# A kernel of two transformer blocks: normed rows turned and split by halves, and the next residual made later on VectorE

## The chip, the cores and the metric

The kernel runs on one core of a Trainium2 chip. The metric is the device time of one execution in microseconds (us). The engines are called as the profile calls them: PE is TensorE (the matmuls), PEld its loads of stationary operands, DVE VectorE, ACT ScalarE, POOL GpSimd, SP SyncE, which issues the DMAs. L408 is line 408 of the kernel before.

## The reference

Two blocks follow each other on one sequence of 512 tokens with 1024 columns. In the first, each of two layers computes `hcat = x @ w_in + b_in`, three attention or gating branches out of it, and then

```python
sub = merged @ w_out + b_out
return layer_norm(DEEPNORM_ALPHA * x + sub, ln_g, ln_b)
```

The second block has two layers of

```python
p = jnp.einsum('btd,dc->btc', h, w_in[l]).astype(F32)
...                                     # four recurrent mixers on p
h = _layer_norm(DN_ALPHA * h + mix, ln1_g[l], ln1_b[l])
f = _swiglu(h, ...)                     # l = 0; a mixture of experts at l = 1
h = _layer_norm(DN_ALPHA * h + f, ln2_g[l], ln2_b[l])
```

So a layer norm stands between any two stages: its result is the input of the next stage's matmuls, and, times `ALPHA` (plus the next layer's `b_out` in the first block), the residual that the next norm adds.

## The kernel before, in words

The rows `H` lie on chip as four row tiles `t` of 128 tokens in two halves `j` of 512 columns, each 128x512 in float32. There are six places at which a norm's result goes into a next stage; I number them by time in the trace: 1, the input of the first layer (from 14.2 us); 2, the second layer (607 us); 3, the mixers of the second block (1192 us); 4, the FFN (`swiglu`, 1620 us); 5, the mixers again (1993 us); 6, the router and experts (2426 us). The last norm goes to the output.

At such a place `norm_rows` does a row tile at a time as its sums arrive: the statistics, the power -0.5 on POOL (L439), and `norm_apply`: the half `j` = 0 in two DVE operations (L467, L468), the half `j` = 1 by ACT (L355), POOL (L470) and DVE (the bias, L485). `norm_end` (L498) then transposes (`norm_transpose`, L495: 32 of 128x128) into seven banks of the accumulator memory and an eighth once one is free, and splits each of the eight transposed columns `k` (128x512) into a high part `hh`, rounded to the matmul's format by ACT (L414), and the rest `hl`, by DVE (L415). After the splits it makes the residual: sixteen multiplications by `ALPHA` at places 1 and 2 (8 each) and eight at each of the others on ACT (L515), and at places 1 and 2 sixteen additions of the bias on POOL (L518) and a store of each into `hd` (SP, L520).

A projection, `proj_f` (L420), takes one bank ("mm", of which there are two) and adds up 24 matmuls of 128x512, three for each `k`: `hh`·`wh`, `hl`·`wh`, `hh`·`wl` (L406, L407, L408). Its operation that reads the bank (the evacuation) is DVE's L592 in the first block, `shift` (ACT L1530, DVE L1532 to L1534) in the mixers, and Silu on ACT (L355) or a DVE multiplication in the FFN. The weights come in chunks of 128x1024 (256 columns, four `k`): a DMA into `wr` (L394), a cast into `wh` by ACT (L395), the rest into `wl` by DVE (L399). A weight of two outputs is thus two chunks, `k` 0 to 3 and `k` 4 to 7. There are four buffers of each.

The order on every engine comes from the framework's scheduler, which takes the program as it is written and puts instructions where it expects them ready; each engine then works strictly in its order. One thing is ordered by hand: in front of a stage, `behind` lets the first `wl` of the next weights go as it will (`FREE = 1`), and orders the next ones behind a split, that of `k` = 3 (`BEHIND`).

Of the kernel before, what the change touches and what calls it, by code (L numbers as in the profile page):

```python
# [314 lines left out]
class K:  # L315
    def __init__(self, ctx, tc, aps):
        self.tc, self.nc, self.aps = tc, tc.nc, aps
        self.ctx = ctx
        pool = lambda name, **kw: ctx.enter_context(tc.tile_pool(name=name, **kw))
        self.cp = pool("cp", bufs=1)  # L320
        self.wp = pool("wp", bufs=2)
        self.xp = pool("xp", bufs=1)
        self.ps = pool("ps", bufs=2, space=PSUM)
        self.dp = pool("dp", bufs=1, space=bass.MemoryType.DRAM)
        nc = self.nc
        x = [[lambda t=t, j=j: self.load(aps["x"][t * P:(t + 1) * P, j * S:(j + 1) * S], "H") for j in range(2)]
             for t in range(4)]
# [12 lines left out]
        nc.vector.memset(self.eps_rms, RMS_EPS)  # L340
        self.mhalf = self.cp.tile([P, 1], F32, name="mhalf")
        nc.vector.memset(self.mhalf, -0.5)
        self.log_exp = False
        self.behind = (None, 0, 0)
        self.hd = [self.dp.tile([S, S], F32, name=f"hd{j}") for j in range(2)]
# [81 lines left out]

    def proj_t(self, w, width, t, hT, kt=KT, tag="mm"):
# [13 lines left out]
    def norm_begin(self, ng, nb, bo=None, keep=None, spill=False, tags="tsatsamt", pool=()):  # L442
# [3 lines left out]
                                  keep=keep, spill=spill, tags=banks, tp={}, pool=pool, late=None,  # L446
# [4 lines left out]
    def norm_rows(self, t, st, apply=True):  # L451
# [4 lines left out]
        with self.tc.issue_after(i):  # L456
            self.norm_late()
        nc.vector.scalar_tensor_tensor(ln.sh[:, t:t + 1], ln.mv[:, t, 0:1], -1.0, ln.rs[:, t:t + 1],
# [31 lines left out]
    def norm_transpose(self, t, ks=range(7)):  # L490
        ln = self.ln
        for k in ks:
            if k not in ln.tp:
                ln.tp[k] = self.bank(ln.tags[k])
            self.nc.tensor.transpose(ln.tp[k][:, t * P:(t + 1) * P], self.H[t][k // 4][:, (k % 4) * P:(k % 4 + 1) * P],  # L495
                                     self.ident)

    def norm_end(self):  # L498

        nc, ln, H = self.nc, self.ln, self.H  # L500
        hh = self.xp.tile([P, KT, S], F32R, name="hh", tag="hh")
        hl = self.xp.tile([P, KT, S], F32R, name="hl", tag="hl")
        for t in range(4):
            self.norm_transpose(t)
        for k in range(KT):
            if k >= 7:
                for t in range(4):
                    self.norm_transpose(t, [k])
            i = self.split(hh[:, k, :], hl[:, k, :], ln.tp[k])
            if k == BEHIND:  # L510
                self.behind = (i.ins, FREE, HELD)
        for t in range(4):
            for j in range(2):
                h = H[t][j]
                nc.scalar.mul(h, h, ALPHA)  # L515
                if ln.bo is not None:
                    with self.tc.issue_after(ln.last_mul):
                        nc.gpsimd.tensor_add(h, h, ln.bo[j])  # L518
                if ln.spill:
                    nc.sync.dma_start(self.hd[j][t * P:(t + 1) * P, :], h)  # L520
        return hh, hl
# [16 lines left out]
    def first_block(self):  # L538
# [6 lines left out]
        for t in range(4):  # L545
            self.norm_apply(t)
            self.norm_late()
        self.ln.bo, self.ln.spill = self.row(R_L + 2), True
# [22 lines left out]
    def hybrid(self, l, hT):  # L571
# [14 lines left out]
        for c in range(0, 12, 2):  # L586
            w = chunk(c)
            for j in range(2):
                o = self.proj_f(w, j * P, hT)
# [3 lines left out]
                                        bcol(c + j), -0.125 if c < 4 else 1.0, op0=ALU.add, op1=ALU.mult)  # L593
        vt = []
# [288 lines left out]
    def second_block(self, hT):  # L883
# [37 lines left out]
        for l in range(DEPTH):  # L921
# [7 lines left out]
            if l == 0:  # L929
                for i in range(2):  # L930
                    hT_ = self.swiglu(hT, aps[f"fgu_{i}"], aps[f"fd_{i}"], (nb + 2, nb + 3) if i else None)
# [181 lines left out]
    def moe(self, hT, norm):  # L1113
# [5 lines left out]
        next(run[0])  # L1119
        next(run[0])  # L1120
        rv = nc.values_load(mi[0:1, 0:1], min_val=0, max_val=S)
        for e in range(8):
            if e == 7:
                self.norm_begin(*norm, keep=[aps["out_0_dram"][0][:, j * S:(j + 1) * S] for j in range(2)], pool=PF)
# [211 lines left out]
    def swiglu(self, hT, wgu, wd, norm):  # L1336
# [3 lines left out]
        for m in range(11):  # L1340
            w = self.weights(wgu[m], KT, CW)
            g = self.proj_f(w, 0, hT)
            s = self.tmp()
            self.act(s, g, AF.Silu)
            u = self.proj_f(w, P, hT)
# [4 lines left out]
        if norm:  # L1350
            self.norm_begin(*norm, spill=True, tags="smsmaatt", pool=PS)
# [24 lines left out]
    def mixers(self, l, hT):  # L1376
# [9 lines left out]
        def feat(t):  # L1386
            if t % 2 == 0:
                hold["w"] = self.weights(wf[t // 2], KT, CW)
            return self.proj_f(hold["w"], (t % 2) * P, hT)
# [650 lines left out]
```

## Time and profile before

| | us |
|---|---|
| median of three runs | 3084.52 (3083.64 to 3090.07) |
| the profiled execution, its time | 3096.13 |
| the profiled execution, its span in the trace | 3094.3 |
| PE busy in that span | 2928.2 |
| DVE busy | 1898.5 |
| ACT busy | 1315.8 |
| POOL busy | 356.0 |

The profiled execution takes 11.6 us (0.4%) more than the median of the runs. The span is what the trace covers; 1.8 us lie around it. The trace gives the start and duration of every instruction, what ended the wait ahead of it, and in any stretch how long each engine worked and which share of full speed TensorE's clock was granted.

### The profile page before, as it was taken

Reading aid. Unit: us, or ns where it says so; the run is one execution under the profiler, and the core shown is the slowest. Engines: PE = TensorE matmul, PEld = TensorE weight load, DVE = VectorE, ACT = ScalarE, POOL = GpSimd, SP = SyncE. Lnnn points to the kernel's source line nnn. Section 1 sums busy time; section 2 is a strip of 40 time slices with the busy share of each in tenths; the row PEclk is TensorE's granted clock in tenths of the full one; section 3 lists DMA queues with packets and bytes.
Section 4 is the critical chain, followed back from the end, with each engine's and each line's share of the span. In section 5 each row is a group of like instructions: output and inputs, shape, how many; then the busy total and the mean of one; then the engine's idle time right before and its main releaser. Section 6 shows DMA issues by size and latency. Waiting matters only on the chain. (4 is left out here: it accounts for less than half of the span.)

```text
span 3094.3 us, 46838 instructions
## 1 busy us (share of the span) xinstructions
PE 2928.2 (95%) x18625; PEld 2410.1 (78%) x18625; DVE 1898.5 (61%) x3408; ACT 1315.8 (43%) x2257; POOL 356.0 (12%) x377
## 2 busy tenths in 40 slices
PE   7999999999999999998999999999989799999986
PEld 5688788887887888786667888778775599989975
DVE  6686554657846566636574233555467677777767
ACT  3534333325433333524443222343254466666653
POOL 3220000112100001004210000100132200000021
PEclk9999999999999999999899999999999899999998
DMA  5322224242222333200303322431012278777774
GB/s 189 104 81 76 69 68 143 83 151 81 73 63 75 115 123 115 86 30 28 103 25 100 94 96 89 133 101 46 29 48 89 96 251 264 255 250 258 249 263 135
DMA packets 116532, 365.65 MB, mean 118 GB/s; under 512 B 13584, under 2 KB 16784, under 8 KB 116304
## 3 DMA queue, kind: packets, MB, share of 16 engines
q1 hardware_dynamic: 113424, 353.13, 35.3%
q0 software_dynamic: 2880, 9.44, 0.9%
q8 instruction: 148, 2.42, 0.3%
q14 instruction: 80, 0.66, 0.1%
HBM read 344.83 MB, written 17.69 MB: 117 GB/s over the span
## 5 line engine op out<-in xcount | busy, mean ns | idle before, releaser
L399 DVE TENSOR_TENSOR wl<-wr,wh 128x1024 fp32r<-128x1024 f32 (+1 forms) x574 | 699.9, 1228 | 517.0 <-ACT wh L395 510.5
L395 ACT CAST wh<-wr 128x1024 fp32r<-128x1024 f32 (+1 forms) x574 | 594.1, 1045 | 725.9 <-PE mm L407 338.7
L406 PE MATMUL mm<-hh,wh 128*128 128x512 f32 (+1 forms) x1616 | 649.7, 402 | 0.1
L407 PE MATMUL mm<-hl,wh 128*128 128x512 f32 (+1 forms) x1616 | 643.5, 398 | 0.0
L408 PE MATMUL mm<-hh,wl 128*128 128x512 f32 (+1 forms) x1616 | 638.6, 396 | 0.1
L406 PEld LDWEIGHTS mm<-hh,wh 128*128 128x128 f32 (+1 forms) x1616 | 305.2, 189 | 74.9 <-issue 6.8
L408 PEld LDWEIGHTS mm<-hh,wl 128*128 128x128 f32 (+1 forms) x1616 | 304.6, 188 | 72.1 <-issue 4.1
L407 PEld LDWEIGHTS mm<-hl,wh 128*128 128x128 f32 (+1 forms) x1616 | 305.2, 189 | 68.7 <-issue 5.9
L1277 PE MATMUL mm<-xgT,wh 128*128 128x320 f32 x704 | 219.6, 312 | 2.4 <-issue 2.4
L1277 PE MATMUL sc<-xgT,wh 128*128 128x320 f32 x704 | 219.2, 311 | 2.7 <-issue 2.7
L1278 PE MATMUL mm<-xgT,wl 128*128 128x256 f32 x704 | 198.0, 281 | 3.7 <-issue 2.7
L1278 PE MATMUL sc<-xgT,wl 128*128 128x256 f32 x704 | 198.9, 283 | 0.7 <-issue 0.6
L407 PE MATMUL mm<-wl,hh 128*128 128x256 f32 x448 | 129.4, 289 | 10.4 <-DVE wl L399 10.4
L1278 PEld LDWEIGHTS mm<-xgT,wl 128*128 128x128 f32 x704 | 134.0, 190 | 4.5 <-issue 2.9
L1277 PEld LDWEIGHTS mm<-xgT,wh 128*128 128x128 f32 x704 | 133.5, 190 | 3.9 <-issue 3.3
L1278 PEld LDWEIGHTS sc<-xgT,wl 128*128 128x128 f32 x704 | 133.5, 190 | 2.7 <-issue 2.7
L1277 PEld LDWEIGHTS sc<-xgT,wh 128*128 128x128 f32 x704 | 133.7, 190 | 1.8 <-issue 1.8
L406 PE MATMUL mm<-wh,hh 128*128 128x256 f32 x448 | 130.2, 291 | 0.0
L439 POOL TENSOR_TENSOR rs<-rs,mhalf 128x1 f32<-128x1 f32 x36 | 29.5, 820 | 874.1 <-DVE rs L438 792.1
L408 PE MATMUL mm<-wh,hl 128*128 128x256 f32 x448 | 129.0, 288 | 0.0
L407 PEld LDWEIGHTS mm<-wl,hh 128*128 128x128 f32 x448 | 86.3, 193 | 13.3 <-DVE wl L399 10.8
L728 DVE TENSOR_REDUCE mn<-sc 128x1 f32<-128x512 f32 x64 | 44.1, 688 | 81.1 <-PE sc L725 80.8
(564 smaller groups left out, 5602.5 us busy)
## 6 DMA issues: line engine op xcount, KB each, us to landing
wr<-mgu SPq DMA_DIRECT2D x176, 512.0 KB
wr<-w SPq DMA_DIRECT2D x172, 512.0 KB
wr<-md SPq DMA_DIRECT2D x88, 512.0 KB
wr<-fgu SPq DMA_DIRECT2D x44, 512.0 KB
wr<-wo SPq DMA_DIRECT2D x32, 512.0 KB
wr<-wbr SPq DMA_DIRECT2D x24, 512.0 KB
row<-rows SPq DMA_DIRECT2D x40, 256.0 KB
wr<-fd SPq DMA_DIRECT2D x20, 512.0 KB
```

What stands on the lines that cost most here:

```text
L395: nc.scalar.copy(hi[:, :n], raw[:, :n])
L399: nc.vector.tensor_sub(lo[:, :n], raw[:, :n], hi[:, :n].bitcast(F32))
L406: mm(out, lh, rh, start=first, stop=False)
L407: mm(out, lh, rl, start=False, stop=False)
L408: mm(out, ll, rh, start=False, stop=last)
L439: self.nc.gpsimd.tensor_tensor(out, out, self.mhalf, op=ALU.pow)
L728: nc.vector.tensor_reduce(mx[u][:, a:a + 1], sc, axis=AX.X, op=ALU.min)
L1277: mm(o[i][:, :2 * CAP], wh, x[:, k, :2 * CAP], start=k == 0, stop=False)
L1278: mm(o[i][:, :256], wl, x[:, k, :256], start=False, stop=k == KT - 1)
```

## The change

`norm_end` becomes two calls of `norm_half`. Half 0 is row tiles 0 and 1 (256 tokens), half 1 tiles 2 and 3. A half has 16 transposes into four banks and four splits, each of two columns `k` at once (128x2x256). Half 0 is written in `norm_rows` of the last row tile, in front of its `sh` and `norm_apply` (at place 1, behind the second tile's `norm_apply`). `behind` now names the last split of half 1. The final norm, which is not transposed, gets `turn=False`.

The first two projections of a stage become one `proj_first`: for each half of the tokens it goes through `k` with both outputs and both weight parts on `hh` (32 matmuls of 128x256), and then with both outputs on `hl` (16), into two banks: 96 matmuls of 128x256 in the place of 48 of 128x512. Both banks are complete only with the last eight of them. Place 6's router stage takes `hT` as before.

The residual is one DVE operation where there is a bias (`h * ALPHA + bo`, 128x512, eight at places 1 and 2), and ACT's multiplication as before where there is none. It is queued in `due` and called by `pay`: in the first block one after each later projection, in the FFN two after each later weight, in the mixers two after each later projection, at place 6 eight at once. POOL's sixteen additions are gone.

```diff
+    def proj_first(self, w, hT):
+        o = [self.bank("mm") for _ in range(2)]
+        hh, hl = hT
+        mm = self.nc.tensor.matmul
+        for n in range(2):
+            ts = slice(n * CW, (n + 1) * CW)
+            for k in range(KT):
+                for j in range(2):
+                    for z in range(2):
+                        mm(o[j][:, ts], w[k][z][:, j * P:(j + 1) * P], hh[:, k, ts], start=k + z == 0, stop=False)
+            for k in range(KT):
+                for j in range(2):
+                    mm(o[j][:, ts], w[k][0][:, j * P:(j + 1) * P], hl[:, k, ts], start=False, stop=k == KT - 1)
+        return o
...
-    def norm_begin(self, ng, nb, bo=None, keep=None, spill=False, tags="tsatsamt", pool=()):
+    def norm_begin(self, ng, nb, bo=None, keep=None, spill=False, tags="ttssaatt", pool=(), turn=True):
...
+        if t == 3 and apply and ln.turn:
+            self.norm_half(0)
...
-    def norm_transpose(self, t, ks=range(7)):
+    def norm_half(self, half):
         ln = self.ln
-        for k in ks:
-            if k not in ln.tp:
-                ln.tp[k] = self.bank(ln.tags[k])
-            self.nc.tensor.transpose(ln.tp[k][:, t * P:(t + 1) * P], self.H[t][k // 4][:, (k % 4) * P:(k % 4 + 1) * P],
-                                     self.ident)
+        if half == 0:
+            ln.hT = [self.xp.tile([P, KT, S], F32R, name=n, tag=n) for n in ("hh", "hl")]
+        tp = [self.bank(ln.tags[4 * half + kp]) for kp in range(4)]
+        for t in (2 * half, 2 * half + 1):
+            for k in range(KT):
+                c = 2 * (k % 2) + t % 2
+                self.nc.tensor.transpose(tp[k // 2][:, c * P:(c + 1) * P],
+                                         self.H[t][k // 4][:, (k % 4) * P:(k % 4 + 1) * P], self.ident)
+        for kp in range(4):
+            hi, lo = (x[:, 2 * kp:2 * kp + 2, half * CW:(half + 1) * CW] for x in ln.hT)
+            i = self.split(hi, lo, tp[kp].rearrange("p (k n) -> p k n", k=2))
+        if half:
+            self.behind = (i.ins, FREE, HELD)
     def norm_end(self):
         nc, ln, H = self.nc, self.ln, self.H
-        hh = self.xp.tile([P, KT, S], F32R, name="hh", tag="hh")
-        hl = self.xp.tile([P, KT, S], F32R, name="hl", tag="hl")
-        for t in range(4):
-            self.norm_transpose(t)
-        for k in range(KT):
-            if k >= 7:
-                for t in range(4):
-                    self.norm_transpose(t, [k])
-            i = self.split(hh[:, k, :], hl[:, k, :], ln.tp[k])
-            if k == BEHIND:
-                self.behind = (i.ins, FREE, HELD)
-        for t in range(4):
-            for j in range(2):
-                h = H[t][j]
+        self.norm_half(1)
+        def residual(t, j):
+            h = H[t][j]
+            if ln.bo is not None:
+                nc.vector.scalar_tensor_tensor(h, h, ALPHA, ln.bo[j], op0=ALU.mult, op1=ALU.add)
+            else:
                 nc.scalar.mul(h, h, ALPHA)
-                if ln.bo is not None:
-                    with self.tc.issue_after(ln.last_mul):
-                        nc.gpsimd.tensor_add(h, h, ln.bo[j])
-                if ln.spill:
-                    nc.sync.dma_start(self.hd[j][t * P:(t + 1) * P, :], h)
-        return hh, hl
+            if ln.spill:
+                nc.sync.dma_start(self.hd[j][t * P:(t + 1) * P, :], h)
+        self.due = [(residual, t, j) for t in range(4) for j in range(2)]
+        return tuple(ln.hT)
+    def pay(self, n=1):
+        for _ in range(min(n, len(self.due))):
+            f, *args = self.due.pop(0)
+            f(*args)
...
+            if t == 1:
+                self.norm_half(0)
...
+            first = self.proj_first(w, hT) if c == 0 else None
             for j in range(2):
-                o = self.proj_f(w, j * P, hT)
+                o = first[j] if first else self.proj_f(w, j * P, hT)
...
+                if c:
+                    self.pay()
...
+        self.pay(8)
...
+            if m == 0 and new:
+                g, u = self.proj_first(w, hT)
+            else:
+                g, u = self.proj_f(w, 0, hT), None
+                self.pay(2)
...
+            u = u or self.proj_f(w, P, hT)
...
+            self.norm_begin(*norm, spill=True, tags="mmaasstt", pool=PS)
...
+                if t == T_R:
+                    hold["o"] = self.proj_first(hold["w"], hT)
+            if t < T_R + 2:
+                return hold["o"][t - T_R]
+            o = self.proj_f(hold["w"], (t % 2) * P, hT)
+            self.pay(2)
```

Beyond the six places the order of instructions on the engines is the same. At three places it is now as follows; the names are those of the text, `H` the rows, `row` a norm's vectors, `mv`, `rs` and `sh` a row tile's statistics, and `tp`, `sc`, `av`, `mm` the banks.

DVE in front of the FFN (place 4), before, from the last row tile's bias on:

```order
L485 TENSOR_TENSOR H<-H,row 128x512
L415 TENSOR_TENSOR hl<-tp,hh 128x512
L415 TENSOR_TENSOR hl<-sc,hh 128x512
L415 TENSOR_TENSOR hl<-av,hh 128x512
L415 TENSOR_TENSOR hl<-tp,hh 128x512
L415 TENSOR_TENSOR hl<-sc,hh 128x512
L415 TENSOR_TENSOR hl<-av,hh 128x512
L415 TENSOR_TENSOR hl<-mm,hh 128x512
L415 TENSOR_TENSOR hl<-tp,hh 128x512
L399 TENSOR_TENSOR wl<-wr,wh 128x1024 x4
```

and after, from the last row tile's `rs` on:

```order
L456 TENSOR_SCALAR rs<-mv 128x1
L505 TENSOR_TENSOR H<-H,row 128x512
L416 TENSOR_TENSOR hl<-sc,hh 128x2x256 x2
L478 SCALAR_TENSOR_TENSOR sh<-mv,rs 128x1
L487 SCALAR_TENSOR_TENSOR H<-H,mv,row 128x512
L488 SCALAR_TENSOR_TENSOR H<-H,rs,row 128x512
L505 TENSOR_TENSOR H<-H,row 128x512
L416 TENSOR_TENSOR hl<-av,hh 128x2x256 x2
L416 TENSOR_TENSOR hl<-tp,hh 128x2x256 x2
L400 TENSOR_TENSOR wl<-wr,wh 128x1024 x4
```

The line numbers of the changed kernel are other ones: L416 is L415, L400 is L399, L478 to L505 are the last row tile's `sh` and `norm_apply`. Half 0's splits have moved ahead of that `norm_apply` (two of them stand in these rows, two ahead of them); half 1's four stand behind it; and the `wl` stand behind all splits, as they did. At place 2 the scheduler also puts four of the eight new residual operations among the last row tile's operations, ahead of half 1's splits; the other four stand behind three `wl`, ahead of the first evacuation.

PE in front of the FFN, before; `wh_14107` and `wl_14108` are the first chunk of the weights, and the 128x128 rows are transposes:

```order
L495 MATMUL sc_14050<-cst_96,H_13260 128x128
L495 MATMUL av_14052<-cst_96,H_13260 128x128
L495 MATMUL mm_14054<-cst_96,H_13260 128x128
L406 MATMUL mm_14118<-hh_14040,wh_14107 128x512
L495 MATMUL tp_14091<-cst_96,H_13248 128x128
L495 MATMUL tp_14091<-cst_96,H_13252 128x128
L495 MATMUL tp_14091<-cst_96,H_13256 128x128
L495 MATMUL tp_14091<-cst_96,H_13260 128x128
L407 MATMUL mm_14118<-hl_14041,wh_14107 128x512
L408 MATMUL mm_14118<-hh_14040,wl_14108 128x512
```

and after, where `wl_14234` is the second chunk (`k` 4 to 7) and `H_13384` to `H_13388` are rows of tiles 2 and 3:

```order
L440 MATMUL mm_14239<-hh_14162,wh_14227 128x256
L440 MATMUL mm_14239<-hh_14162,wl_14228 128x256
L440 MATMUL mm_14238<-hh_14162,wh_14233 128x256
L519 MATMUL tp_14200<-cst_96,H_13384 128x128 x2
L519 MATMUL tp_14201<-cst_96,H_13384 128x128 x2
L440 MATMUL mm_14239<-hh_14162,wh_14233 128x256
L519 MATMUL av_14198<-cst_96,H_13386 128x128 x2
L519 MATMUL av_14199<-cst_96,H_13386 128x128 x2
L519 MATMUL tp_14200<-cst_96,H_13388 128x128 x2
L519 MATMUL tp_14201<-cst_96,H_13388 128x128 x2
L440 MATMUL mm_14238<-hh_14162,wl_14234 128x256
L440 MATMUL mm_14239<-hh_14162,wl_14234 128x256
```

Eighteen matmuls of the first half of the tokens (of which ten stand in these rows) now stand ahead of the last transposes, and the next one takes `wl_14234`.

ACT at the first mixers (place 3), before, from the next to last split on:

```order
L414 CAST hh<-av 128x512
L414 CAST hh<-mm 128x512
L414 CAST hh<-tp 128x512
L515 ACTIVATE H<-H 128x512 x5
L1530 COPY tmp<-mm 128x512
L395 CAST wh<-wr 128x1024 x2
L1530 COPY tmp<-mm 128x512 x2
L395 CAST wh<-wr 128x1024 x2
```

and after, from the last row tile's `norm_apply` on:

```order
L538 ACTIVATE H<-H 128x512 x5
L415 CAST hh<-av 128x2x256 x2
L415 CAST hh<-tp 128x2x256 x2
L538 ACTIVATE H<-H 128x512 x2
L396 CAST wh<-wr 128x1024
L1573 COPY tmp<-mm 128x512 x2
L396 CAST wh<-wr 128x1024
L1573 COPY tmp<-mm 128x512
```

A cast of a later weight now stands ahead of the first `COPY`, the evacuation of the first projection, and that `COPY` has a second one right behind it.

## Rows read from the trace of the kernel before

**Rows 1.** The page: busy time, share of the span, instructions of each engine.

```profile
PE 2928.2 (95%) x18625; PEld 2410.1 (78%) x18625; DVE 1898.5 (61%) x3408; ACT 1315.8 (43%) x2257; POOL 356.0 (12%) x377
```

**Rows 2.** PE's waits: what released it, us in total, times, longest.

```profile
PE sc L495 <- DVE H L485: 15.8, 11, 3.2
```

**Rows 3.** Windows, places 1 to 5: length, busy PE PEld DVE ACT POOL, PEclk, DMA, GB/s.

```profile
14.20:41.57 27.37, 21.89 (x80) 16.26 (x81) 26.10 (x44) 14.84 (x24) 21.82 (x15) 1.00 0.47 167
606.95:629.18 22.23, 17.61 (x82) 14.12 (x81) 19.88 (x25) 11.47 (x20) 16.34 (x11) 0.85 0.31 109
1192.21:1213.38 21.17, 16.88 (x82) 13.67 (x81) 17.24 (x27) 12.06 (x21) 5.82 (x7) 0.92 0.60 196
1619.58:1642.71 23.13, 17.72 (x82) 14.40 (x81) 16.82 (x24) 14.09 (x23) 3.18 (x3) 0.85 0.27 91
1993.19:2015.39 22.20, 17.44 (x81) 13.74 (x80) 17.97 (x27) 12.26 (x21) 5.42 (x7) 0.85 0.56 189
```

**Rows 4.** Timeline of DVE: start, us, operation; first `wl` behind the splits, places 1 to 5.

```profile
24.86 2.29 DVE L399 TENSOR_TENSOR wl<-wr,wh 128x1024 fp32r<-128x1024 f32 x1
...
620.10 3.44 DVE L399 TENSOR_TENSOR wl<-wr,wh 128x1024 fp32r<-128x1024 f32 x2
...
1204.71 2.76 DVE L399 TENSOR_TENSOR wl<-wr,wh 128x1024 fp32r<-128x1024 f32 x2
...
1632.83 0.68 DVE L415 TENSOR_TENSOR hl<-tp,hh 128x512 fp32r<-128x512 f32 x1
1633.43 2.35 DVE L399 TENSOR_TENSOR wl<-wr,wh 128x1024 fp32r<-128x1024 f32 x2
...
2006.85 2.34 DVE L399 TENSOR_TENSOR wl<-wr,wh 128x1024 fp32r<-128x1024 f32 x2
```

**Rows 5.** Timeline in front of the FFN: the last row tile, one split.

```profile
1621.56 1.66 ACT L515 ACTIVATE H<-H 128x512 f32<-128x512 f32 x3
...
1624.31 0.93 POOL L439 TENSOR_TENSOR rs<-rs,mhalf 128x1 f32<-128x1 f32 x1 [4.12 <-DVE rs L438]
...
1625.46 0.81 ACT L355 ACTIVATE H<-H,sh,rs 128x512 f32<-128x512 f32 x1 [2.23 <-DVE sh L458]
...
1626.35 1.65 POOL L470 TENSOR_TENSOR H<-H,row 128x512 f32<-128x512 f32 x1 [1.12 <-ACT H L355]
...
1628.03 0.69 DVE L485 TENSOR_TENSOR H<-H,row 128x512 f32<-128x512 f32 x1 [1.16 <-POOL H L470]
...
1628.64 0.68 DVE L415 TENSOR_TENSOR hl<-tp,hh 128x512 fp32r<-128x512 f32 x1
```

**Rows 6.** Windows of narrow matmuls, of place 3 and of place 5.

```profile
1186.77:1192.20 5.43, 5.43 (x50) 5.43 (x49) 4.69 (x9) 3.68 (x4) 2.66 (x2) 1.00 0.00 2
1200.60:1203.20 2.60, 2.60 (x10) 2.23 (x9) 2.60 (x5) 2.46 (x5) 0.43 (x1) 0.50 0.00 0
1998.50:2005.30 6.80, 4.20 (x14) 2.95 (x14) 5.60 (x9) 6.50 (x13) 4.46 (x5) 0.50 0.65 246
2005.30:2015.39 10.09, 10.09 (x45) 8.29 (x44) 7.60 (x10) 2.06 (x3) 0.00 (x0) 1.00 0.60 208
```

**Rows 7.** Timeline: evacuations and what lies beside them, first block, mixers, FFN.

```profile
645.86 1.21 DVE L592 TENSOR_SCALAR naqkv<-mm,vec 128x512 f32<-128x512 f32 x1 [3.21 <-PE mm L408]
...
1209.92 0.59 ACT L1530 COPY tmp<-mm 128x512 f32<-128x512 f32 x1 [4.45 <-PE mm L408]
...
1210.65 1.05 ACT L395 CAST wh<-wr 128x1024 fp32r<-128x1024 f32 x1
...
1211.33 0.75 DVE L1534 SCALAR_TENSOR_TENSOR sh<-sh,vec,mm 128x512 f32<-128x512 f32 x1
...
1211.99 1.22 DVE L399 TENSOR_TENSOR wl<-wr,wh 128x1024 fp32r<-128x1024 f32 x1
...
1634.21 1.28 ACT L355 ACT_TABLE_LOAD   x1
1639.25 0.60 ACT L355 ACTIVATE tmp<-mm 128x512 f32<-128x512 f32 x1 [3.75 <-PE mm L408]
```

More of the change, by code (lines that the diff above doesn't have):

```diff
@@ L344, in __init__ @@
         self.behind = (None, 0, 0)
+        self.due = []
         self.hd = [self.dp.tile([S, S], F32, name=f"hd{j}") for j in range(2)]
@@ L440, in rstd_col @@
         return i.ins
-    def norm_begin(self, ng, nb, bo=None, keep=None, spill=False, tags="tsatsamt", pool=()):
+    def norm_begin(self, ng, nb, bo=None, keep=None, spill=False, tags="ttssaatt", pool=(), turn=True):
         banks = [{"t": "tp", "s": "sc", "a": "av", "m": "mm"}[c] for c in tags]
         self.ln = SimpleNamespace(g=self.row(ng), b=self.row(nb), bo=None if bo is None else self.row(bo),
-                                  keep=keep, spill=spill, tags=banks, tp={}, pool=pool, late=None,
+                                  keep=keep, spill=spill, tags=banks, turn=turn, pool=pool, late=None,
                                   mv=self.xp.tile([P, 4, 2], F32, name="mv", tag="mv", bufs=2),
@@ L930, in second_block @@
                 for i in range(2):
-                    hT_ = self.swiglu(hT, aps[f"fgu_{i}"], aps[f"fd_{i}"], (nb + 2, nb + 3) if i else None)
+                    hT_ = self.swiglu(hT, aps[f"fgu_{i}"], aps[f"fd_{i}"], (nb + 2, nb + 3) if i else None, i == 0)
                 hT = hT_
@@ L1123, in moe @@
             if e == 7:
-                self.norm_begin(*norm, keep=[aps["out_0_dram"][0][:, j * S:(j + 1) * S] for j in range(2)], pool=PF)
+                self.norm_begin(*norm, keep=[aps["out_0_dram"][0][:, j * S:(j + 1) * S] for j in range(2)], pool=PF, turn=False)
                 last = self.choose(pos, g)
@@ L1334, in expert, with swiglu @@
             put(rest_col * P + own, R, j, t[:R])
-    def swiglu(self, hT, wgu, wd, norm):
+    def swiglu(self, hT, wgu, wd, norm, new):
         nc = self.nc
@@ L1341, in swiglu @@
             w = self.weights(wgu[m], KT, CW)
-            g = self.proj_f(w, 0, hT)
+            if m == 0 and new:
[3 more added lines that the diff above has]
+                self.pay(2)
             s = self.tmp()
             self.act(s, g, AF.Silu)
-            u = self.proj_f(w, P, hT)
+            u = u or self.proj_f(w, P, hT)
             nc.vector.tensor_mul(s, s, u)
@@ L1350, in swiglu @@
         if norm:
-            self.norm_begin(*norm, spill=True, tags="smsmaatt", pool=PS)
+            self.norm_begin(*norm, spill=True, tags="mmaasstt", pool=PS)
             st = self.xp.tile([P, 4, 2, 6], F32, name="st2", tag="st2", bufs=2)
@@ L1388, in feat @@
                 hold["w"] = self.weights(wf[t // 2], KT, CW)
-            return self.proj_f(hold["w"], (t % 2) * P, hT)
+                if t == T_R:
[4 more added lines that the diff above has]
+            self.pay(2)
+            return o
         def tok(i, out):
```

## The prediction

> **What bounds the kernel now.** I read the page's busy times first: PE works 2928.2 us of the span, 95%, the next engine 61% [rows 1]. So PE's stream is the time, and a shift of it at one place persists to the end, unless PE waits later for something that has not shifted. PE's waits come next: the largest one with a cause inside the kernel is its wait for the last operation of a row tile's norm (DVE's bias, L485), 15.8 us in eleven waits, the longest 3.2 [rows 2]. These are the places that the change works on. Windows over them, each from a norm's last transposes to the start of the third projection, show 22.2, 21.2, 23.1 and 22.2 us at places 2 to 5, of which PE is busy 17.6, 16.9, 17.7 and 17.4 [rows 3]. Idle are thus 4.6, 4.3, 5.4 and 4.8 us, 19.1 in all; place 1 has 5.5. PE's busy time there holds some work at half clock: the mean granted clock is 0.85 to 0.92 [rows 3], and the stretch inside place 5 where PE waits has 0.50 [rows 6].
>
> What ends such a place is not the transposes but DVE. It makes eight splits at a pace of 0.60 us (0.599 from the first to the last start, seven steps) [rows 4, 5] and then the `wl` for `k` 4 to 7. PE, which takes its order as it stands, can't finish its first projection without that `wl`. I call its end W: half of the pair behind its start, so 620.10 + 1.72 = 621.8 at place 2, 1206.1 at 3, 1634.6 at 4 and 2008.0 at 5 [rows 4]. From W to the end of the window PE still has 7.4, 7.3, 8.1 and 7.4 us of the two projections, 30.2 together; the rest of them it did ahead of W.
>
> **The first two projections, places 2 to 5.** The order shows the weak point. In the changed kernel PE has 16 matmuls of the first half of the tokens on chunk `k` 0 to 3 and two on the next, and then needs the `wl` for `k` 4 to 7, which DVE makes behind the splits of both halves. So 78 of 96 narrow matmuls lie behind W. A wide one takes 10.09 / 45 = 0.224 us [rows 6], a narrow one half of that, 0.112: 78 x 0.112 = 8.74 us at a place, 34.9 at four. Against 30.2 that is **+4.7**, were W where it was.
>
> W moves a little. At the FFN the half-0 splits ahead of the last `rs` put the power on POOL (0.93) 1.2 us later; two more splits, and multiplications by `ALPHA` that now stand in front of ACT's part of the norm (0.55 each, 1.66 for three), make that part start 1.9 to 2.7 later than 1625.46. POOL's 1.65 and DVE's bias follow at the same distance [rows 5]. Behind the bias stood eight splits, and there stand two, as two of half 1's fit into the wait for POOL: six times 0.60, 3.6 us, less, but the last tile's transposes and first cast (about 1 us, the cast at 0.59 as ACT's `COPY` of the same size [rows 7]) are not covered by earlier splits any more. That gives W between 0.9 and 0.1 earlier; I take 0.3. The same walk gives 0.4 at place 2 (where four residual operations stand in DVE's way, but POOL's additions no longer slow the `wl` pair, 3.44 against 2.34), 1.1 at 3 and 0.9 at 5, **-2.7** together. Bounds: 2.4 earlier at each (half 0's four splits vanish into DVE's waits), -9.6, or no earlier at all, 0.
>
> **The clock, same places.** PE is idle until W now, and the dense work begins there. In place 3 there is a stretch of 2.60 us in which PE was busy throughout and the granted clock was still 0.50 [rows 6], the 1.2 GHz level. Before, this recovery lay ahead of W: place 5 is dense and at full clock from 2005.30, 2.7 us ahead of its W [rows 4, 6]. Behind W such a stretch costs half of itself, 1.3 us: four times, **+5.2**. Bounds: 0 (the eighteen early matmuls and the transposes keep the clock) to 8 (the recovery takes 1.5 times as long).
>
> **The handover to the third projection.** This is new. Two "mm" banks are there, and both become complete with the last eight matmuls, so the third projection waits until the first of them has been read out. Before, the second projection's 5.4 us (24 x 0.224) covered that reading. At place 2 it is one DVE operation of 1.21 [rows 7] and about 0.2 for two engines to take over from each other (0.08 from ACT's end 1626.27 to POOL's start 1626.35 [rows 5]): **+1.4**. In the mixers the order puts a weight's cast (1.05) ahead of the first `COPY`; its buffer comes free with eight matmuls to go, 0.9, so it ends 0.15 late. DVE then has that chunk's `wl` (1.22) ahead of `shift`, whose chain from the start of the `COPY` to the end of its last operation takes 1212.08 - 1209.92 = 2.16, 1.57 of it behind the `COPY`; the second bank's subtraction (about 0.6) stands in between [rows 7]. 0.15 + 1.22 + 1.57 + 0.6 + 0.2 = 3.75, at places 3 and 5: **+7.5**. At the FFN the cast's 0.15, a table load that the order has moved behind it (1.28), Silu 0.60 and 0.2 [rows 7]: 2.2, with another 0.2 for the release, **+2.4**. Together +11.3. Bounds: without cast, `wl` and table load in the way 1.4 + 2 x 2.36 + 0.8 = 6.9; with one more `wl` at each mixer place 13.7.
>
> The Trainium skill speaks against this part: "Perfetto Trace Analysis", section "Matmuls", asks that independent matmul groups rotate through different PSUM banks, so that reading one out overlaps the next group. By that rule every place pays a reading-out, as the sum above has it from rows. The same section holds larger matmuls to be more efficient; a window of 50 narrow ones in 5.43 us, 0.109 each, shows no such loss against half of 0.224 [rows 6], and the measurement decides: nothing is charged for width.
>
> **The residual.** POOL's sixteen additions and eight of the sixteen blocked stores on SP at place 2 had PE as cover and bound nothing; they go for nothing. The new DVE operations behind later weights have PE's dense projections as cover (DVE is at 61%), **0**; if that cover is gone, at place 2 the four that stand ahead of the first evacuation cost up to 4 x 0.75 (as the same operation of `shift` [rows 7]) = 3 us less the 8.7 - 2.4 us that DVE has until it: still nothing.
>
> **Place 1** had DVE busy 26.10 of 27.37 us and POOL 21.82 [rows 3], and a `wl` took 2.29 there against 1.2 [rows 4]. It gains some 1.8 from the `wl` and splits without POOL's additions, and pays a handover of 1.4: **-0.4**, bounds -2 to +3. **Place 6** needs every `hl` for its router at once: **0**, bounds -1 to +1.
>
> **The sum:** 4.7 - 2.7 + 5.2 + 11.3 - 0.4 = +18.1 us on the profiled execution's 3096.1. That execution stands 11.6 above the median of the runs, which lies in no place that changes, so I put the same difference on the median: 3084.5 + 18.1 = **3102.6**. What a measurement of this kernel can tell from no change is about 0.2%, 6.2 us.
>
> **Rivals.**
> A, faster: half 0 really fills the waits. The place is DVE's wait for POOL in the last tile's norm. If all half-0 splits vanish there, W comes 2.4 earlier at each place (4.7 - 9.6 = -4.9); if the early matmuls also hold the clock, the half-speed stretch goes too, in which PE was busy 4.20 us [rows 6], 2.1 each, -8.4; and the handovers come at their lower bound, 6.9. -4.9 - 8.4 + 6.9 - 0.4 = -6.8: 3078. It decides at the last tile's transposes: they must not start later than before. ACT's multiplications ahead of the norm speak against it, DVE's wait of 1.16 ahead of the bias [rows 5] for it.
>
> B, no change: W moves by 2.4, the clock costs nothing and the handovers 6.9: -4.9 + 6.9 - 0.4 = +1.6, 3086. For it: the early matmuls are work that PE didn't have there. Against it: 18 of them are 2 us in a wait of five.
>
> C, slower still: W stays, the recovery costs 8, the handovers 13.7: 4.7 + 8 + 13.7 - 0.4 = 26: 3110.6. For it: the last tile's chain goes through three engines, each with new work ahead.
>
> D, the change doesn't do what it says: the scheduler puts residual operations in front of the norm, as at place 2 it does with four. If the bias there comes their 3 us later, +3 on the forecast, 3105.6; this lies within its range.
>
> **How the numbers follow.** The forecast has 0.55 with D in it (3092 to 3108), C 0.15, B 0.18, A 0.12. Faster by over 0.2% is A alone, and slower are the forecast and C; B is the middle. The range leaves out A and the outer ends of B and C: 3085 to 3112.
>
> **What would show it.** In the changed trace: a wait of PE of 1 to 4 us ahead of the third projection of each of the places 1 to 5, released by `naqkv`, `shift` and Silu; none of these, and the handover term is wrong. A first-half stretch of 18 matmuls, then idle until the `wl` for `k` 4 to 7; if PE runs on through `k` 4 to 7 ahead of the last transposes, rival A is right. W within 1 us of 621.8, 1206.1, 1634.6 and 2008.0 by the place's own start. The granted clock still 0.5 some 2.6 us behind W. The windows of places 3 and 5 longer by about 5 us, those of 2 and 4 by 3 to 4. Outside the places, all as it was; a time lost there would be one that I have not seen.

## The result, and the profile after

The changed kernel takes 3109.2 us (median of four runs, 3105.1 to 3111.7), the kernel before 3084.2 beside it: a ratio of 1.0076, 95% interval 1.0062 to 1.0091. It is slower by 25 us; 18 had been forecast. The profiled execution of the changed kernel took 3111.7.

The page of the changed kernel, its span and the busy times as in [rows 1]:

```profile
span 3109.9 us, 47303 instructions
...
PE 2932.3 (94%) x18865; PEld 2427.8 (78%) x18865; DVE 1897.8 (61%) x3424; ACT 1306.4 (42%) x2241; POOL 326.5 (10%) x361
```

PE is busy for 4 us longer: the same work is cut into 240 more and shorter matmuls (five times 96 in the place of 48). The span grew by 15.6. (This span is set against that of an execution before which stood 11.6 above its median; what that is, is told below.) PE's waits of the changed kernel, in the columns of [rows 2]:

```profile
PE mm L440 <- DVE wl L400: 12.7, 5, 3.5
...
PE tp L519 <- DVE H L505: 10.8, 7, 4.0
PE av L519 <- DVE H L488: 10.4, 5, 3.2
...
PE mm L407 <- DVE sh L1576: 7.0, 2, 3.5
...
PE mm L407 <- DVE naqkv L622: 2.2, 2, 1.1
PE mm L407 <- ACT tmp L356: 2.1, 1, 2.1
```

The first row is new: PE waits 12.7 us for a `wl` ahead of the narrow matmuls (L440). The last three are new too: the first wide matmul of the third projection (L407) waits for what reads the joint projections' banks, 7.0 + 2.2 + 2.1 = 11.3 us. The waits of the last row tile's transposes stay (L519). The timeline of PE shows the third projection's first matmul at places 1 to 5, and in brackets its wait:

```profile
39.79 0.51 PE L407 MATMUL mm<-hh,wh 128*128 128x512 f32 x1 [1.12 <-DVE naqkv L622]
...
632.31 0.50 PE L407 MATMUL mm<-hh,wh 128*128 128x512 f32 x1 [1.12 <-DVE naqkv L622]
...
1225.40 0.77 PE L407 MATMUL mm<-hh,wh 128*128 128x512 f32 x1 [3.50 <-DVE sh L1576]
...
1663.43 0.50 PE L407 MATMUL mm<-hh,wh 128*128 128x512 f32 x1 [2.15 <-ACT tmp L356]
...
2043.90 0.47 PE L407 MATMUL mm<-hh,wh 128*128 128x512 f32 x1 [3.51 <-DVE sh L1576]
```

Against the ends of [rows 3] this start is 1.8 us earlier at place 1, and 3.1, 12.0, 20.7 and 28.5 later at places 2 to 5. PE's matmuls in between stand in the same order in both traces; matched one by one, their distance changes far less inside a stage than at a place: -2.0 in front of place 2, 5.5 in front of 3, 15.0 in front of 4, 20.9 in front of 5. So the places themselves add 5.1, 6.5, 5.7 and 7.6 us, 24.9 together, and the stages between them 5.4, of which 1.6 lie right behind the handover of place 3. The other 3.8 come in steps of under 0.6 us in the stages behind places 2 and 3; their cause is not shown. Further on the distance is 26.4 us in front of place 6.

Windows from the second `wl` (PE's wait for it ends there) to the last matmul of the joint projections, places 2 to 5, columns as in [rows 3]:

```profile
619.65:631.20 11.55, 11.54 (x78) 11.34 (x78) 4.70 (x7) 0.87 (x1) 0.00 (x0) 0.80 0.69 227
1210.50:1221.90 11.40, 11.39 (x78) 11.19 (x78) 2.23 (x2) 0.86 (x1) 0.00 (x0) 0.81 0.48 155
1649.10:1661.30 12.20, 12.15 (x78) 11.94 (x78) 2.25 (x2) 0.88 (x1) 0.00 (x0) 0.75 0.40 130
2028.40:2040.40 12.00, 11.96 (x78) 11.76 (x78) 2.25 (x2) 0.86 (x1) 0.00 (x0) 0.77 0.43 135
```

Each holds 78 matmuls, all of them dense, and each has a mean granted clock of 0.75 to 0.81. At the FFN the same in pieces, first the last row tile's last transposes, ahead of the wait for the `wl`, and at the end the stretch behind the handover of place 5:

```profile
1645.20:1646.40 1.20, 1.08 (x4) 0.71 (x4) 1.20 (x3) 0.70 (x2) 0.00 (x0) 0.50 0.00 0
1646.40:1649.10 2.70, 0.03 (x1) 0.00 (x0) 2.50 (x5) 1.24 (x3) 0.00 (x0) 0.50 0.00 0
1649.10:1655.10 6.00, 5.97 (x28) 5.97 (x29) 2.25 (x2) 0.00 (x0) 0.00 (x0) 0.50 0.70 221
1655.10:1661.30 6.20, 6.18 (x52) 5.97 (x51) 0.00 (x0) 0.88 (x1) 0.00 (x0) 1.00 0.11 43
2043.90:2047.30 3.40, 3.40 (x9) 2.68 (x10) 1.71 (x2) 0.00 (x0) 0.00 (x0) 0.56 0.36 96
```

The clock is at half already in those transposes, so it fell in PE's waits for the last row tile. PE then does nothing for 2.7 us (the wait for the `wl`), then works without a gap for 6.0 us at half clock, 28 matmuls of 0.21, and only then at full clock, 52 of 0.12 (two on the edges count in both windows). At places 2, 3 and 5 the first 4.65, 4.30 and 5.60 us behind the `wl` are at 0.50 too. Behind the 3.5 us of the handover of place 5 the clock is at half again for most of 3.4 us.

The handover at the first mixers (place 3), timeline of ACT and DVE:

```profile
1221.04 1.05 ACT L396 CAST wh<-wr 128x1024 fp32r<-128x1024 f32 x1 [11.73 <-issue]
...
1221.99 1.06 ACT L1573 COPY tmp<-mm 128x512 f32<-128x512 f32 x2
1222.12 1.23 DVE L400 TENSOR_TENSOR wl<-wr,wh 128x1024 fp32r<-128x1024 f32 x1 [9.39 <-ACT wh L396]
...
1223.26 0.68 DVE L1575 TENSOR_TENSOR sh<-tmp,mm 128x511 f32<-128x511 f32 x1
...
1223.92 0.68 DVE L1575 TENSOR_TENSOR sh<-tmp,mm 128x511 f32<-128x511 f32 x1
1224.52 0.74 DVE L1577 SCALAR_TENSOR_TENSOR sh<-sh,vec,mm 128x512 f32<-128x512 f32 x1
```

The last narrow matmul ends at 1221.9. ACT's cast runs until 1222.09 and so past it, the two `COPY` follow, DVE makes that chunk's `wl` first (1222.12), then two subtractions and the operation (L1577) that frees the first bank, at 1225.26; PE goes on at 1225.40.

### The profile page after: what moved, and what is told of

It is laid out like the page before. It is cut to its first block, busy times and chain, and to the rows that moved or that the text cites. A ratio compares the mean times of both kernels' runs of the same rounds, so it can differ in the third digit from the quotient of the medians.

```text
span 3109.9 us, 47303 instructions
## 1 busy us (share of the span) xinstructions
PE 2932.3 (94%) x18865; PEld 2427.8 (78%) x18865; DVE 1897.8 (61%) x3424; ACT 1306.4 (42%) x2241; POOL 326.5 (10%) x361
## 5 line engine op out<-in xcount | busy, mean ns | idle before, releaser
L400 DVE TENSOR_TENSOR wl<-wr,wh 128x1024 fp32r<-128x1024 f32 (+1 forms) x574 | 695.9, 1221 | 532.6 <-ACT wh L396 520.3
L407 PE MATMUL mm<-hh,wh 128*128 128x512 f32 (+1 forms) x1536 | 617.4, 402 | 11.5 <-DVE sh L1576 7.0
L409 PE MATMUL mm<-hh,wl 128*128 128x512 f32 (+1 forms) x1536 | 608.2, 396 | 0.0
L408 PE MATMUL mm<-hl,wh 128*128 128x512 f32 (+1 forms) x1536 | 608.2, 396 | 0.0
L407 PEld LDWEIGHTS mm<-hh,wh 128*128 128x128 f32 (+1 forms) x1536 | 289.2, 188 | 80.8 <-issue 14.1
L409 PEld LDWEIGHTS mm<-hh,wl 128*128 128x128 f32 (+1 forms) x1536 | 288.9, 188 | 69.1 <-issue 4.0
L408 PEld LDWEIGHTS mm<-hl,wh 128*128 128x128 f32 (+1 forms) x1536 | 289.0, 188 | 66.7 <-issue 5.9
L408 PE MATMUL mm<-wl,hh 128*128 128x256 f32 x448 | 129.6, 289 | 10.3 <-DVE wl L400 10.3
L407 PE MATMUL mm<-wh,hh 128*128 128x256 f32 x448 | 130.4, 291 | 0.0
L408 PEld LDWEIGHTS mm<-wl,hh 128*128 128x128 f32 x448 | 86.8, 194 | 13.2 <-DVE wl L400 10.8
```

The lines of the kernel that those rows point to most:

```text
L400: nc.vector.tensor_sub(lo[:, :n], raw[:, :n], hi[:, :n].bitcast(F32))
L407: mm(out, lh, rh, start=first, stop=False)
L408: mm(out, lh, rl, start=False, stop=False)
L409: mm(out, ll, rh, start=False, stop=last)
```

## The experiments

Banks apart, the second `wl` free, projections apart and the residual alone ran on one chip; both edits together, the kernel before with joint projections and the two further runs with the second `wl` free on a second; the twelve matmuls, the changed kernel beside them and both edits again on a third. Each is compared with runs of the kernel before on its own chip. On the second the kernel before spread from 3081 to 3105 us, and the intervals there are wider.

**Banks apart.** In the second half of the tokens the joint projections do one output after the other:

```diff
-            for k in range(KT):
-                for j in range(2):
+            for js in ((0, 1),) if n == 0 else ((0,), (1,)):
+                for k in range(KT):
+                    for j in js:
...
```

> The changed kernel, with one edit: in the second half of the tokens the two outputs of the joint first projections are done one after the other, so that the first bank is complete 24 narrow matmuls (2.7 us) ahead of the second. All else as in the changed kernel, whose runs are at 3109.2. Theory (the handover with both banks complete at once costs its PE waits, 1.1 + 1.1 + 3.5 + 2.2 + 3.5 = 11.4 us in the trace, and the half clock that follows it at two places, 1.7 each): the waits at places 1 and 2 vanish and at 3 to 5 fall by 2.7 at most, to 0.8, 0 and 0.8, so 3109 - 9.8 - 3.4 = 3096 (3093 to 3100). Rival (PE's wait there is only moved, since DVE's and ACT's queues hold the evacuation back by the weight's cast and wl whatever the banks do): 3106 to 3110, with the same waits ahead of the third projection.

Measured: 3098.1 us, 1.0044 of the kernel before (1.0028 to 1.0061), so 10 to 11 less than the changed kernel. PE at the end of the joint projections of place 3, in the timeline:

```profile
1218.11 0.40 PE L407 MATMUL mm<-hh,wh 128*128 128x512 f32 x1
```

The third projection starts without a wait. The three rows of waits of L407 that made 11.3 us are gone from PE's waits, at the mixers too, where 0.8 had been expected to stay; PE's wait for the second `wl` stays, 12.0 us in four. The time lies in the theory's range, 2 us above its middle, and the rival, by which the waits would only move, is out. At place 3 the edit also takes the cast out of the way: the cast waits for the last narrow matmuls (1217.88), while ACT's `COPY` of the first bank goes at 1215.48, and DVE has read that bank out at 1217.6.

**Second `wl` free.**

```diff
-FREE = 1
+FREE = 2
```

> The changed kernel with FREE = 2 instead of 1: the wl of the second chunk (k 4 to 7) may stand ahead of the splits, and at the FFN it does so by the order. Theory (PE idles until that wl because it stands behind all splits, and has 78 of 96 narrow matmuls left then): PE does the 48 matmuls of the first half of the tokens in its waits for the last row tile, and 48 x 0.112 = 5.4 us are left behind the last split instead of 8.7 behind a wl that comes 1.2 later. Gain 4.5 at each of places 2 to 5, less 1.2 each for the wl ahead of the last tile, and 1 to 2 each of half clock: 3109 - 13 - 6 = 3090 (3085 to 3097). The waits ahead of the third projection stay at some 11 us. Rival (the last tile's chain over DVE, POOL and ACT decides, and a wl in front of it only moves it): 3106 to 3112.

Measured: 3084.4, 0.9998 (0.9988 to 1.0008): the whole loss is gone, although the handovers are all there, as PE's waits show:

```profile
PE mm L407 <- DVE sh L1576: 7.0, 2, 3.5
...
PE mm L407 <- DVE naqkv L622: 2.4, 2, 1.3
...
PE mm L407 <- ACT tmp L356: 2.1, 1, 2.1
...
PE mm L440 <- DVE wl L400: 0.3, 1, 0.3
```

The wait for the `wl` fell from 12.7 to 0.3. The windows of the FFN, ahead of the last tile's transposes and behind them:

```profile
1615.40:1624.40 9.00, 7.43 (x59) 6.71 (x57) 8.12 (x15) 6.53 (x13) 2.25 (x2) 1.00 0.37 118
1625.30:1632.10 6.80, 6.62 (x55) 6.46 (x55) 4.83 (x7) 2.95 (x5) 0.00 (x0) 1.00 0.24 73
```

Of the 96 narrow matmuls 45 now lie ahead of the last tile's last transposes. With these transposes the other 51 go at a granted clock of 1.00 and take 6.8 us, where the changed kernel took 12.2 from its second `wl` on. So this edit gave more than the 19 us at the theory's middle, and the time came out just below its range: the half clock, taken with 1 to 2 us at each place, went altogether from behind the last splits (the windows behind the last transposes show 1.00 at all of places 2 to 5). It now stands behind the handovers, in the third projection. At place 3:

```profile
1209.97:1216.20 6.23, 6.23 (x15) 4.93 (x16) 1.71 (x2) 0.00 (x0) 0.00 (x0) 0.53 0.25 84
```

At places 4 and 5 the granted clock is 0.67 in the first 5.1 us there.

**Both.** 

> The changed kernel with both edits: the second wl free (FREE = 2, alone 3084.4) and the banks of the second half one after the other (alone 3098.1, 11.1 less than the changed kernel). Theory (two separate losses: PE idle until the second wl, and the handover with its half clock): the gains add, 3084.4 - 11.1 = 3073 (3069 to 3078), faster than the kernel before; PE's waits ahead of the third projection 0 at places 1, 2 and 4 and at most 1 at 3 and 5, and no half clock behind them. Rival (once the clock is up and PE starts early, the handover is hidden or its gain is the same one as the wl's): 3080 to 3086.

Measured: 3076.0, 0.9956 (0.9937 to 0.9974). PE's waits ahead of the third projections are gone, at the mixers too. It ran once more on the third chip, as follows.

> The changed kernel with the second wl free and the banks apart, again and with more rounds: 0.44% under the kernel before, as it was (0.3 to 0.6), and so 1.2% (37 us) under the changed kernel.

Measured: 3068.2, 0.9948 (0.9934 to 0.9961). It is faster than both kernels: by 14 to 16 us than the one before. The changed kernel took 3116.4 on that chip (see below), 48 us (1.4%) more, where 37 had been expected. The gains add: 0.42% to 0.5% more than the free `wl` alone, where banks apart had given 0.3% to 0.4%. The FFN's windows in the first of the two (3076.0), the joint projections and what follows:

```profile
1616.40:1625.00 8.60, 8.45 (x64) 8.12 (x65) 6.48 (x9) 6.18 (x9) 0.00 (x0) 1.00 0.35 114
1625.00:1633.00 8.00, 8.00 (x37) 6.57 (x36) 2.49 (x4) 1.99 (x3) 0.00 (x0) 1.00 0.41 139
```

Both at a clock of 1.00, and PE busy for 8.45 of 8.60 and 8.00 of 8.00 us.

**Projections apart.** The two projections as in the kernel before, the halves and the residual as changed: `proj_first` returns two `proj_f`.

> The changed kernel with its first two projections as in the kernel before (24 wide matmuls each, one output after the other), the halves of the turn and split and the residual as changed. Theory (the loss lies in the joint projections: what they leave behind the second wl, their handover and the clock): about the kernel before less the 2.7 us by which the wl come earlier, 3082 (3078 to 3088). Rival (the splits in front of the last tile's norm and ACT's multiplications delay the norm itself, and this is the loss): 3095 to 3105.

Measured: 3085.0, 0.9997 (0.9987 to 1.0008). The loss lies in the joint projections; the split in halves, placed in front of the last tile's norm, costs nothing by itself that can be told, nor does it gain (the 2.7 us expected of it are too few to be seen here).

**The residual alone**, in the kernel before:

> The kernel before with the changed residual alone: one DVE operation in the first block (no POOL additions), called behind later projections. Theory (the residual is covered by PE's dense work): no change, 3084 (3080 to 3088). Rival (DVE's additional operations or the later stores delay evacuations or weights): 3090 or more.

Measured: 3084.3, 0.9996 (0.9985 to 1.0007). No change, as expected.

**The kernel before with joint projections**, wide, `k` by `k`:

```diff
...
+        for k in range(KT):
+            for j in range(2):
+                self.mm3(o[j], w[k][0][:, j * P:(j + 1) * P], w[k][1][:, j * P:(j + 1) * P], hh[:, k, :], hl[:, k, :], k == 0, k == KT - 1)
...
```

> The kernel before with one edit: the first two projections of a stage run jointly, k by k, three wide matmuls for one output and then three for the other, so that both banks are complete within 0.7 us of each other; turn, splits, wl and residual as before. Theory (the handover costs by itself, wherever PE waited ahead of it): waits ahead of the third projection of 0.4 at places 1 and 2, 2.8 at 3 and 5, 1.5 at 4, and half clock behind the longer ones (1.7 each): 3086 + 8 to 11.5 = 3096 (3092 to 3099). Rival (in the kernel before DVE's and ACT's queues are not held by a cast and wl there, so that the handover is hidden): 3083 to 3089.

Measured: 1.0026 (1.0010 to 1.0043), 8 us more than the kernel before. The handover costs there too, as the waits show, but less than in the changed kernel:

```profile
PE mm L406 <- DVE sh L1551: 3.1, 2, 1.6
...
PE mm L406 <- DVE naqkv L602: 1.8, 2, 1.3
```

The mixers' waits are 1.6 and not 2.8; those of places 1 and 2 are 1.3 and 0.6 and not 0.4, and at place 4 PE has none. Together they are 4.9 us, where 7.9 had been expected, and the clock behind the mixers' waits stays at 1.00. The waits thus account for 4.9 of the 8 us; where the rest lies is not shown. The timeline of ACT and DVE at place 3 tells why the mixers' are shorter:

```profile
1218.22 0.59 ACT L1547 COPY tmp<-mm 128x512 f32<-128x512 f32 x1 [3.57 <-PE mm L408]
...
1218.73 1.04 ACT L395 CAST wh<-wr 128x1024 fp32r<-128x1024 f32 x1
...
1219.62 0.75 DVE L1551 SCALAR_TENSOR_TENSOR sh<-sh,vec,mm 128x512 f32<-128x512 f32 x1
...
1220.43 0.50 PE L406 MATMUL mm<-hh,wh 128*128 128x512 f32 x1 [1.55 <-DVE sh L1551]
```

Here the `COPY` goes ahead of the cast and no `wl` stands in front of `shift`: its chain takes 2.15 us from the `COPY` to the end of L1551, PE waits for 1.55 of them. Of the two further microseconds of the changed kernel's wait, 0.8 lie ahead of the `COPY`: it starts 0.1 us behind the end of the last matmul and not 0.7 ahead of it, as the cast stands in front and the banks end closer together. The other 1.1 lie in the chain, which takes 3.27 us from the `COPY` on, with the `wl` and the second bank's subtraction in it. The direction is the theory's, the size its lower end.

**The kernel before with the second `wl` free**, and **the halves with projections apart and the second `wl` free**.

> The kernel before with FREE = 2: the second wl ahead of the eight splits. Theory (without halves PE has nothing to do in the wait, and the matmuls follow the splits): what stands behind the last split falls by the wl's 1.2 us, and the norm comes 1.2 later where DVE's wl stands ahead of it: 3086 (3081 to 3089). Rival (the place of the wl alone is worth what it was worth in the changed kernel, some 25 us): 3062 to 3075.

> The changed kernel with the first two projections as before (one output after the other, 24 wide matmuls each; alone 3085.0) and the second wl free. Theory (a wide matmul needs both halves of the tokens, so PE has nothing to do on half 0 alone): 3083 (3079 to 3086), no more than the 1.2 us that the wl comes earlier at each place. Rival (the halves with the early wl gain by DVE's order, whatever PE does): 3075 or less.

Measured: 1.0013 (0.9995 to 1.0031), no difference that can be told, and 1.0025 (1.0007 to 1.0043), 8 us more than the kernel before. The second is outside of what was expected. What the traces show of it: PE's waits ahead of the last tile's transposes at the FFN, first with the `wl` held (projections apart, above) and then with it free.

```profile
1624.10 1.08 PE L507 MATMUL tp<-cst,H 128*128 128x128 f32 x4 [3.94 <-DVE H L493]
```

```profile
1631.14 1.08 PE L507 MATMUL tp<-cst,H 128*128 128x128 f32 x4 [4.95 <-DVE H L493]
...
1635.72 1.12 PE L507 MATMUL tp<-cst,H 128*128 128x128 f32 x4 [0.85 <-DVE H L493]
```

The first wait has grown by 1.0 us and another of 0.85 has come: the `wl` stands ahead of the last tile's statistics and puts them off by its 1.2, and wide matmuls give PE nothing to do in that time. Between these two traces places 2 to 5 grow by 0.7, 1.8, 1.4 and 1.3 us, 5.2 together. The second trace is of the slowest of ten executions (3114.8, their median is 3099.6), so the 8 us are not fully traced. In neither of the two runs does the early `wl` gain; in the runs here it gained only together with matmuls that need no more than half 0.

**Twelve more matmuls in the wait**, into a bank that nobody reads, and the changed kernel beside it:

```diff
...
+                        if fill and (n, k, j, z) == (0, 4, 0, 1):
+                            d = self.bank("sc")
+                            for i in range(12):
+                                mm(d[:, :CW], w[i % 4][0][:, :P], hh[:, i % 4, :CW], start=i == 0, stop=i == 11)
...
```

> The changed kernel with one addition: at each place twelve more narrow matmuls (128x256, 0.11 us each at full clock, 0.22 at half) into a spare bank that nobody reads, in the order behind the eighteenth matmul and ahead of the one that waits for the second wl, so that they lie in PE's waits for the last row tile or for that wl. Theory (part of the loss is that PE's idle time ahead of the wl leaves the granted clock at half for 4 to 6 us of the dense work behind it, some 10 us at places 2 to 5 in the trace): the half clock ends earlier, 3 to 8 us less than the changed kernel beside it. Rival (the clock follows something else than PE's own work there): within 2 us of it, or 2 to 5 more where the twelve put off the last transposes.

> The changed kernel itself, beside the other on the same chip: 0.76% over the kernel before, as it was (0.6 to 0.9).

Measured: 3111.4, 1.0085 (1.0071 to 1.0099), against 3116.4, 1.0092 (1.0076 to 1.0108). The medians lie 5 us apart, the intervals overlap: as a time it is inconclusive. The changed kernel came out at 0.92%, just above what had been expected of it (0.6 to 0.9). The windows of the 78 matmuls at places 2 to 5, with the twelve:

```profile
619.70:631.00 11.30, 11.30 (x78) 11.14 (x78) 4.63 (x7) 0.81 (x1) 0.00 (x0) 0.81 0.72 233
1210.20:1221.20 11.00, 10.98 (x78) 10.78 (x78) 2.23 (x2) 0.86 (x1) 0.00 (x0) 0.84 0.51 162
1645.90:1657.80 11.90, 11.88 (x78) 11.68 (x78) 2.19 (x2) 0.88 (x1) 0.00 (x0) 0.77 0.42 132
2024.70:2033.80 9.10, 9.09 (x78) 8.89 (x78) 2.20 (x2) 0.83 (x1) 0.00 (x0) 1.00 0.54 174
```

and without them, on the same chip:

```profile
620.40:632.50 12.10, 12.10 (x78) 11.90 (x78) 4.68 (x7) 0.85 (x1) 0.00 (x0) 0.75 0.66 217
1212.40:1223.90 11.50, 11.43 (x78) 11.22 (x78) 2.26 (x2) 0.89 (x1) 0.00 (x0) 0.81 0.51 156
1646.50:1657.70 11.20, 11.17 (x78) 10.97 (x78) 2.20 (x2) 0.89 (x1) 0.00 (x0) 0.83 0.46 142
2026.40:2037.10 10.70, 10.70 (x78) 10.51 (x78) 2.21 (x2) 0.84 (x1) 0.00 (x0) 0.87 0.45 150
```

At place 5, where the twelve stand right ahead of the waiting matmul, the 78 go at 1.00 and take 9.1 us; in the two executions without them they take 10.7 and, above, 12.0. This is not shown to be the twelve's work, since the clock differs before they begin. They come behind the last row tile's transposes, and PE's wait ahead of these shows, first in the changed kernel (the trace of the result) and then with the twelve:

```profile
2023.00:2024.60 1.60, 0.05 (x1) 0.00 (x0) 1.10 (x2) 1.47 (x3) 1.60 (x3) 0.75 0.36 134
```

```profile
2019.50:2021.10 1.60, 0.04 (x1) 0.00 (x0) 1.11 (x2) 1.46 (x3) 1.60 (x3) 1.00 0.37 138
```

Without the twelve the clock falls in that wait; with them it has not fallen yet when they start. At places 2 to 4 most of the twelve stand ahead of the last transposes, with a wait of some 3 us behind them, and there the change is -0.8, -0.5 and +0.7, no more than between two executions of the changed kernel (12.2 and 11.2 at place 4). So the traces show what full clock is worth at place 5, 1.6 to 2.9 us; whether work of PE's own in the wait brings it stays open.

## Why the prediction was right, and where its size was off

The direction and the mechanisms came as forecast: much work left behind the second `wl`, part of it at half clock, and a handover to the third projection. By its steps:

- **What is left behind the second `wl`.** 78 of 96 matmuls, as read from the order: the windows count x78 at all four places. The price was a little low: 78 at full clock take 9.1 us (place 5 with the twelve), and not 8.74. The forecast divided a window by its 45 matmuls, though its edges cut the outer ones; in the timelines wide ones start 0.23 us apart and narrow ones 0.118.
- **Where W lies.** -2.7 was forecast. Measured at W, by the second `wl` (its start and a third of its three, 619.5, 1210.4, 1649.0 and 2028.3) against [rows 4] and the distance in front of each place: -0.3, -1.2, -0.6 and -0.6, -2.7 together. At place 3 that is just over the 1 us which the forecast had set as a sign.
- **The clock** is the term that was mis-sized: +5.2 with an upper bound of 8. The four windows take 47.2 us; at full clock they would take 4 x 9.1 = 36.4. That is 10.8. The forecast took the length of the half clock from a stretch of 2.60 us in the kernel before [rows 6]; in the changed kernel PE's idle time reaches to W itself, and the stretch behind it lasts 4.65, 4.30, 6.00 and 5.60 us. The FFN of the kernel before had a longer stretch than 2.60 to read, busy throughout and at half clock:

```profile
1628.80:1633.20 4.40, 4.40 (x14) 3.73 (x15) 4.40 (x8) 4.40 (x10) 0.00 (x0) 0.50 0.00 0
```

- **The handover.** +11.3 at places 2 to 5, measured 1.12 + 3.50 + 2.15 + 3.51 = 10.3, and at the mixers by the chain that was written down: cast, `wl`, two subtractions, L1577. What it does to the clock was left out: behind the two long ones (places 3 and 5) the distance grows by another 1.6 and 1.7 us.
- **Place 1**: -0.4 forecast, -1.8 measured. **The residual**: nothing, as the run of it alone shows.

For places 2 to 5 the forecast was 2.0 + 5.2 + 11.3 = 18.5, measured 24.9; the clock makes up 5.6 of the 6.4, the price of the narrow matmuls 1.5, and the handovers take 1.0 back. These places grew by 5.1, 6.5, 5.7 and 7.6 us, where 3 to 5 had been named as the sign. The forecast had nothing for the stages between them, which add 5.4. That the places' 24.9 and the 25 between the medians are nearly equal is thus in part chance: at the third projection of place 5 the distance is 28.5 us, in front of place 6 26.4.

- **The profiled execution and the median.** I put the sum on the median, since the 11.6 us between the two executions lie in no place that changes. The traces bear this out. At 2998.7 us, in the experts, the changed kernel is 25.1 us behind; over the matmuls that follow, the distance falls to 14.0. These are the same matmuls, first in the kernel before and then in the changed one:

```profile
2998.70:3018.90 20.20, 11.46 (x40) 9.53 (x40) 9.65 (x19) 6.81 (x13) 8.16 (x9) 0.58 0.79 277
```

```profile
3023.80:3032.90 9.10, 7.14 (x43) 6.91 (x42) 7.58 (x16) 4.59 (x10) 7.27 (x7) 0.81 1.03 398
```

The profiled execution of the kernel before takes 11.1 us more there, about what it stands above its median. This is why the spans differ by 15.6 and the medians by 25.
- **The rivals.** A (half 0 fills the waits) fell where the forecast had put its point: the `wl` stands behind the splits. Its own sign failed too: the FFN's last transposes come 1.6 us later than before (1645.32 against 1628.78, less the distance of 15.0). Put ahead, the kernel does what A describes, and with the banks apart it is faster than the kernel before. B fell with it. C was nearer to the truth in one term, the clock (its 8 was still low), and not in the others: the handovers and W came as in the forecast.

The Trainium skill's "Perfetto Trace Analysis", section "Matmuls", asks for independent matmul groups to rotate through different PSUM banks, so that one is read out while the next runs. The trace agrees: two groups in two banks that end together cost 11.3 us of PE's waits, and ending them 24 matmuls apart took all of it away. Its preference for larger matmuls shows faintly in the trace: narrow matmuls start 0.118 us apart, half of a wide one's 0.23 is 0.115, and over 96 of them that is 0.3 us at a place.

## What to carry to other kernels

Work that is made ready early fills a wait only as far as its last operand goes: read on the order which instruction of the waiting engine comes first that needs something late, and look there, not at the data that was split. Joint accumulation over two banks puts both read-outs at the same end; let one bank finish earlier, and look at what is queued ahead of its read-out (24 narrow matmuls were enough here, as the read-out then also stood ahead of the cast). And count the clock behind PE's waits: here it cost some 10 us at four places where PE waited 12 for the `wl`, and 1.6 and 1.7 behind two waits of 3.5.

## What the runs showed that I had not expected

The half clock was as dear as the wait that I had counted: at the FFN PE waits 2.7 us for the `wl`, and then does 6.0 us of dense work at half clock, which is 3.0 us. That wait did not bring the clock down, though: it was at 0.50 already in the transposes ahead of it. And the last stage, from place 6 to the end of its matmuls, took 646.0 and 638.0 us in two executions of one kernel, the one with both edits, on two chips: 8 us, which is half of what this change could have been worth.
